# Earlier set-up, paired gates and early merge products in a transformer-layer kernel

## The chip, the cores and the metric

The kernel runs on one core of a Trainium2 chip. It is timed in microseconds of device time. The engines are TensorE (PE, matrix products), VectorE (DVE), ScalarE (ACT), GpSimd (POOL) and SyncE (SP, which here only issues DMAs).

## The reference

One layer of a trunk on an input of 512 x 1024 float32. The layer normalizes x to h, projects h by one matrix whose columns are shared by three branches and three gates, runs the branches, and merges them; an output projection and a gated feed-forward block follow. Cut to what matters here:

```python
h = rms_norm(x, g)
z = h @ w_in                       # columns: A (attention), B (S5), C (delta rule), gates
ya = dsa_attention(...) @ w_proj_a # index scores, top-k keys, attention
yb = s5_branch(...) @ w_proj_b     # complex diagonal scan: A_bar = exp(dt * a), B_bar from it
yc = gated_delta_rule(...) @ w_proj_c  # per chunk of 64: a triangular system is inverted
y = sum(sigmoid(gate_i) * y_i)     # the merge, a 512 x 1024 gate for each branch
x = x + y @ w_out
x = x + ffn(rms_norm(x, g2))
out = rms_norm(x, g_final)
```

Products are exact to about float32: each factor is split into a high and a low part of a reduced format (`wh`, `wl` and `hh`, `hl`), and three partial products are summed.

## The kernel before

**Products.** A product of 128 output columns is 8 slices of k by 3 partial products, that is 24 matmuls 128x512 (12 for a merge, whose k is 512). `wload` (L275 ff.) loads a weight tile by SyncE's queue into a staging tile `w` (two of them), casts it to `wh` on ScalarE (L258) and subtracts to `wl` on VectorE (L259). There are two pairs `wh`, `wl`; a third pair (`wx`) serves some of the 20 first products after the front. `proj` takes the next product from a queue of weights that are loaded up to three ahead. The PSUM tags are `acc` (2 buffers), `sm` (2), `pt` (3) and `po` (1).

**Order.** The program is written as generators (`topk`, `gates`, `s5_main`, `merge` and others) which strings and rates weave into one order. A scheduler with a model of the engines then orders each engine's queue; `issue_after` holds an instruction behind another in that order.

**Front.** Inputs come in by SyncE's queue. ScalarE and VectorE split the raw input into `xh`, `xl`; ScalarE squares x for the norm; the norm's factor goes through a power on GpSimd, a small product, and a copy on ScalarE to `rB`, one row broadcast to all partitions (L368). Four products of the raw input (`pu`), and a product of 76 columns for the index key (`index_in`, PSUM tag `acc`), need no norm; they are scaled by `rB` afterwards (L1448, L751). The normalized, transposed input is made in eight slices: `ht` by VectorE from `rB` (L1465), `hh` by ScalarE, `hl` by VectorE. Then come the gates: one product each, `m_th` = tanh of the accumulator by ScalarE (L1296), stored to `gd`. The set-up of S5 (`s5_setup`) is a generator of three steps: dt and the reduced angle; the magnitude, sine and cosine (L415 to L443) with a table load on ScalarE; and the discretized matrices. The first step stands before the products, the second is issued as the last weight of the front is there (`lastw`), the third follows in the weave.

**Exchange.** The delta rule inverts triangular blocks on VectorE, step by step (L928 to L938), writes the blocks to DRAM and gathers them block by block into `g_X` and its transpose `g_Y`, four gathers each, all on SyncE's queue (L959). The products from `g_X` (in tag `sm`) start the second level of the inverse. TensorE's filler around it are products of gates, and the first products of the merge of branch B (`merge`), which use the tag `acc`.

**Tail.** For each of four row blocks the sums of squares of the two halves are added, scaled, raised to −1/2 on GpSimd; ScalarE scales the first half, VectorE the second, and SyncE stores both.

Of the kernel before, what the change touches and what calls it, by code (L numbers as in the profile page):

```python
# [163 lines left out]
IL = 1  # L164
PI = 2
SE = 1
# [61 lines left out]
class _K:  # L228
# [46 lines left out]
    def wload(self, src, n=1024, hl=None, extra=False):  # L275
        nc = self.nc
        w = self.wp.tile([128, 1024], F32, tag="w", name="w", bufs=2)
        nc.sync.dma_start(w[:, :n], src)
        self.wi += 1
# [13 lines left out]
    def dense(self, ps, wh, wl, xh, xl, nk, c0=0, cs=128, m=128, t=slice(0, 512)):  # L293
        for k in range(nk):
# [4 lines left out]
            self.mm(ps[:, t], b, xh[:, k, t], False, k == nk - 1)  # L299
# [29 lines left out]
    def ahead(self, n):  # L329

        while len(self.fq) < n and self.fpos < len(PLAN):
# [3 lines left out]
            w = self.wload(self.I["w_in"][i], extra=self.fpos <= N_WX)  # L335
# [3 lines left out]
    def proj(self, i):  # L339
# [6 lines left out]
        return ps  # L346

# [38 lines left out]
    def s5_setup(self):  # L386
# [35 lines left out]
        tt(t1, t1, t1, OP.mult)  # L422
        nc.vector.tensor_scalar(cs, t1, -2.0, 1.0, OP.mult, OP.add)
# [57 lines left out]
    def s5_half(self, hf):  # L481
# [17 lines left out]
        E = self.s5e.tile([128, 8, 2, 64], F32, tag="b4", name="s5_b4", bufs=2)  # L499
        for ri, (x1, y1, x2, y2, op) in enumerate(((ar, bb[0], ai, bb[1], OP.subtract), (ar, bb[1], ai, bb[0], OP.add))):  # L500
# [3 lines left out]
            tt(e, e, u2, op)  # L504
        cre3 = v3("cre")
# [238 lines left out]
    def index_in(self, xh, xl):  # L744
# [3 lines left out]
        ps = self.acc()  # L748
# [46 lines left out]
    def gdn_main(self):  # L795
# [167 lines left out]
        for h0 in (0, 2):  # L963
            ps = self.acc("sm")
            P1 = [P1h(), P1h()]
            for h in range(2):
                nc.gpsimd.memset(half(P1[h], 1), 0.0)
                for t in range(4):
                    c = slice(t * 128, (t + 1) * 128)
                    o_ = h * 256 + t * 64  # L970
                    self.mm(ps[:, o_:o_ + 64], NT[:, h0 + h, c], half(XF[:, h0 + h, c], 0))
# [186 lines left out]
    def attn(self):  # L1158
# [17 lines left out]
        def keys(j):  # L1176
# [113 lines left out]
    def gates(self, n0, n1):  # L1290
        nc = self.nc
        for n in range(n0, n1):
            gd = self.dp.tile([128, 512], F32, tag="gd%d" % n, name="gd%d" % n, bufs=1)
            pg = self.proj(W_GA + n)
# [6 lines left out]
    def merge(self, wname, gate0, br, prev=None, dst=None):  # L1301
# [3 lines left out]
        for n2 in range(4):  # L1305
            ph, pl = self.wload(self.I[wname][n2])
            for j in range(2):
# [6 lines left out]
                ps = self.acc()  # L1314
                self.dense(ps, ph, pl, bh, bl, 4, c0=j * 512)
# [13 lines left out]
    def run(self):  # L1329
# [10 lines left out]
        self.gd, self.md = {}, {}  # L1340
        self.gpi, self.gpw = False, False
        self.wx, self.wi = None, 0
# [5 lines left out]
        with ExitStack() as mix:  # L1348
# [13 lines left out]
            with ExitStack() as s:  # L1362
                self.s5s = s.enter_context(self.pool("s5s", bufs=1))
# [18 lines left out]
                lsq, wst0 = [], []  # L1382

# [5 lines left out]
                def ld(c):  # L1389
# [25 lines left out]
                    else:  # L1415
                        with self.tc.issue_after(lsq[-1].ins) if lsq else ExitStack():
                            ws[n] = self.wload(I["w_in"][W_U + n])

                for i, c in enumerate(XO.split(',')):
                    ld(c)  # L1420
                    if i == PI:
                        sync(self.par[:, :64], I["par"][:, :64])
                        setup = self.s5_setup()
                        if SE == 0:
                            next(setup)
                sync(self.ident, I["const"][:, :128])
                if SE == 1:
                    next(setup)
# [15 lines left out]
                for n in range(4):  # L1444
                    if n % 2 == 0:
                        us = sqt()
# [3 lines left out]
                if SE == 2:  # L1450
                    next(setup)
# [5 lines left out]
                if not IL:  # L1457
                    self.index_in(xh, xl)
# [10 lines left out]
                if IL:  # L1469
                    self.index_in(xh, xl)  # L1470
# [3 lines left out]
                self.wx = s.enter_context(self.pool("wx", bufs=1))  # L1474
# [4 lines left out]
                drain(_weave(_chain(setup, self.s5_main()), fill, R_S5))  # L1479
# [184 lines left out]
```

## Time and profile before

| | us |
|---|---|
| median of 3 runs | 943.15 (941.37 to 944.28) |
| the profiled execution | 942.5 |
| its span | 940.7 |
| TensorE busy in it | 910.5 (97%) |
| VectorE busy | 642.9 (68%) |
| ScalarE busy | 415.3 (44%) |

The chain that ended last lies 77% of the span on TensorE, 12% on VectorE, 3% on ScalarE. The rows that the prediction uses stand in their own section below. In a row of a timeline the two first numbers are the start and the duration in microseconds; then come engine, line, operation, the tile written and the tiles read, the shape, a count, and in brackets how long the engine was idle before it and what released it. A matmul is pipelined, and starts before the one ahead has ended.

### The profile page before, as it was taken

Reading aid. Unit: us, or ns where it says so; the run is one execution under the profiler, and the core shown is the slowest. Engines: PE = TensorE matmul, PEld = TensorE weight load, DVE = VectorE, ACT = ScalarE, POOL = GpSimd, SP = SyncE. Lnnn points to the kernel's source line nnn. Section 1 sums busy time; section 2 is a strip of 40 time slices with the busy share of each in tenths; the row PEclk is TensorE's granted clock in tenths of the full one; section 3 lists DMA queues with packets and bytes.
Section 4 is the critical chain, followed back from the end, with each engine's and each line's share of the span. In section 5 each row is a group of like instructions: output and inputs, shape, how many; then the busy total and the mean of one; then the engine's idle time right before and its main releaser. Section 6 shows DMA issues by size and latency. Waiting matters only on the chain.

```text
span 940.7 us, 12731 instructions
## 1 busy us (share of the span) xinstructions
PE 910.5 (97%) x4804; PEld 744.1 (79%) x4804; DVE 642.9 (68%) x1132; ACT 415.3 (44%) x753; POOL 59.5 (6%) x99
## 2 busy tenths in 40 slices
PE   8899999998999999899999999999999999999996
PEld 6677877787888787788777889888888888888885
DVE  5879889789998779347678545866666666522423
ACT  6475453335575643258744224543444344321212
POOL 2221001110003100200100000000000000000000
PEclk9999999999999999899999999999999999999999
DMA  8485234532225545532137513422322322232312
GB/s 325 147 203 175 73 101 124 154 139 101 90 91 153 148 120 178 134 131 73 46 127 233 210 45 113 134 90 90 111 91 90 108 93 90 90 112 90 96 61 90
DMA packets 49677, 114.55 MB, mean 122 GB/s; under 512 B 15696, under 2 KB 16080, under 8 KB 49488
## 3 DMA queue, kind: packets, MB, share of 16 engines
q1 hardware_dynamic: 42256, 97.74, 32.1%
q0 software_dynamic: 3904, 9.70, 4.3%
q10 hardware_dynamic: 3456, 6.29, 1.8%
q8 instruction: 38, 0.62, 0.3%
q14 instruction: 23, 0.19, 0.1%
HBM read 94.84 MB, written 14.42 MB: 116 GB/s over the span
## 4 chain that ended last, share of the span: by engine, by line
PE 77%; DVE 12%; issue 3%; ACT 3%; DMA 3%; SPq 0%; POOL 0%; ACTq 0%; POOLq 0%; DVEq 0%
PE ps_acc L250 40%; PE ps_sm L250 20%; PE ps_pt L250 11%; PE ps_po L250 4%; DVE a_wk L1111 1%; DVE wl L259 1%; PE ps_pt L253 1%; DVE a_m L1110 1%; PE ps_sm L253 1%; DMA w<-in_w_in_dram 1%; ACT wh L258 1%; DMA xt<-in_xt_dram 1%; DVE ht L1465 1%; DVE s_rb L688 0%; DMA s_yT<-s_yd 0%
## 5 line engine op out<-in xcount | busy, mean ns | idle before, releaser
L259 DVE TENSOR_TENSOR wl<-w,wh 128x1024 fp32r<-128x1024 f32 (+1 forms) x140 | 168.8, 1207 | 142.9 <-ACT wh L258 142.8
L258 ACT CAST wh<-w 128x1024 fp32r<-128x1024 f32 (+1 forms) x140 | 145.4, 1039 | 220.8 <-PE ps_acc L250 120.1
L250 PE MATMUL ps_acc<-hh,wh 128*128 128x512 f32 x376 | 150.8, 401 | 5.4 <-ACT m_th L1296 2.8
L250 PE MATMUL ps_acc<-hh,wl 128*128 128x512 f32 x376 | 148.6, 396 | 0.9 <-DVE wl L259 0.9
L250 PE MATMUL ps_acc<-hl,wh 128*128 128x512 f32 x376 | 148.2, 395 | 1.0 <-DVE hl L259 1.0
L250 PEld LDWEIGHTS ps_acc<-hh,wh 128*128 128x128 f32 x376 | 71.1, 189 | 22.6 <-ACT m_th L1296 4.0
L250 PEld LDWEIGHTS ps_acc<-hh,wl 128*128 128x128 f32 x376 | 71.0, 189 | 17.1 <-DVE wl L259 1.3
L250 PEld LDWEIGHTS ps_acc<-hl,wh 128*128 128x128 f32 x376 | 71.1, 189 | 15.9 <-DVE hl L259 1.5
L250 PE MATMUL ps_acc<-f_hh,wh 128*128 128x512 f32 x160 | 62.3, 389 | 0.0
L250 PE MATMUL ps_acc<-f_hl,wh 128*128 128x512 f32 x160 | 62.3, 389 | 0.0
L250 PE MATMUL ps_acc<-f_hh,wl 128*128 128x512 f32 x160 | 62.2, 389 | 0.0
L250 PE MATMUL ps_sm<-f_hh,wh 128*128 128x512 f32 x160 | 62.2, 389 | 0.0
L250 PE MATMUL ps_sm<-f_hl,wh 128*128 128x512 f32 x160 | 62.2, 389 | 0.0
L250 PE MATMUL ps_sm<-f_hh,wl 128*128 128x512 f32 x160 | 62.2, 389 | 0.0
L258 ACT CAST ah<-f_th 128x512 fp32r<-128x512 f32 x22 | 13.6, 620 | 57.6 <-DVE f_th L1600 57.6
L250 PEld LDWEIGHTS ps_acc<-f_hh,wl 128*128 128x128 f32 x160 | 30.0, 188 | 6.3
L250 PEld LDWEIGHTS ps_sm<-f_hh,wh 128*128 128x128 f32 x160 | 30.0, 188 | 6.3
L250 PEld LDWEIGHTS ps_acc<-f_hh,wh 128*128 128x128 f32 x160 | 30.1, 188 | 6.2
L250 PEld LDWEIGHTS ps_sm<-f_hl,wh 128*128 128x128 f32 x160 | 30.1, 188 | 6.2
L250 PEld LDWEIGHTS ps_sm<-f_hh,wl 128*128 128x128 f32 x160 | 30.0, 188 | 6.2
L250 PEld LDWEIGHTS ps_acc<-f_hl,wh 128*128 128x128 f32 x160 | 30.0, 187 | 6.1
L1598 ACT ACTIVATE f_th<-f_a 128x512 f32<-128x512 f32 x22 | 13.9, 633 | 45.2 <-DVE f_a L1595 45.2
(538 smaller groups left out, 1944.7 us busy)
## 6 DMA issues: line engine op xcount, KB each, us to landing
w<-in_w_in_dram SPq DMA_DIRECT2D x50, 512.0 KB, 3.4
w<-in_w_up_dram SPq DMA_DIRECT2D x44, 512.0 KB, 3.4
w<-in_w_down_dram SPq DMA_DIRECT2D x22, 512.0 KB, 3.2
gd<-m_th ACTq DMA_DIRECT2D x24, 256.0 KB, 2.7
m_th<-gd SPq DMA_DIRECT2D x24, 256.0 KB, 3.2
w<-in_w_out_dram SPq DMA_DIRECT2D x8, 512.0 KB, 4.0
sq<-in_x_dram SPq DMA_DIRECT2D x4, 512.0 KB, 9.5
w<-in_w_proj_b_dram SPq DMA_DIRECT2D x4, 512.0 KB, 3.6
```

What stands on the lines that cost most here:

```text
L250: return self.nc.tensor.matmul(out, lhsT, rhs, start=start, stop=stop)
L253: return self.nc.tensor.transpose(out, in_, self.ident[base:base + n, base:base + n])
L258: self.lasta = nc.scalar.copy(hi, src)
L259: self.lastv = nc.vector.tensor_sub(lo, src, hi.bitcast(F32))
L1110: nc.vector.max(m8, wk[:, :N])
L1111: nc.vector.match_replace(wk[:, :N], m8, wk[:, :N], SENT)
L1465: nc.vector.scalar_tensor_tensor(h, xs[k // 2][:, k % 2], ag[:, k:k + 1], self.rB, OP.mult, OP.mult)
L1598: nc.scalar.activation(th, tl[0], AF.Tanh)
```

## The change

- `s5_setup`: the second step stands right behind the first inputs. Its magnitude no longer waits for the front's weights, its sines stand behind the third square of x, and half the angle's sine has a tile of its own. The third step is issued behind the last slice of h.
- A third pair of weight tiles (`wx`) exists from the start and serves the third front weight and the gates 0, 3, 6 and so on; every third staging tile comes from a pool of its own (`w3`).
- The two first gates are one function, `proj_pair`, which goes through k once for both.
- The index product accumulates in the tag `sm`, and stands behind the slices of h; the scaled `pu` products are stored two before and two behind it.
- Exchange: the gathers of `g_Y` go by GpSimd's queue; the zeros of the attention keys (`a_kl`) stand behind them; the first three products of the first merge accumulate in `pt`, and the first products from `g_X` are held behind them.
- Tail: the scale and the small constant are applied to the first half's sum when it is there, and the second half is added in one step; the first half of the output is shared by ScalarE (352 columns, its own DMA) and VectorE (160).

```diff
@@ wload
-        w = self.wp.tile([128, 1024], F32, tag="w", name="w", bufs=2)
+        self.wi += 1
+        if self.w3 and self.wi % 3 == 0:
+            w = self.w3.tile([128, 1024], F32, tag="w3", name="w", bufs=1)
+        else:
+            w = self.wp.tile([128, 1024], F32, tag="w", name="w", bufs=2)
         nc.sync.dma_start(w[:, :n], src)
-            if self.wx and extra and self.fpos % 3 == 0:
+            if self.wx and extra:
@@ ahead
-            w = self.wload(self.I["w_in"][i], extra=self.fpos <= N_WX)
+            w = self.wload(self.I["w_in"][i], extra=self.fpos <= N_WX and self.fpos % 3 == 1)
+    def proj_pair(self, i):
+        self.ahead(2)
+        two, pss = [self.fq.pop(0) for _ in range(2)], [self.acc(), self.acc()]
...
+        for k in range(8):
+            c = slice(k * 128, k * 128 + 128)
+            for ps, q in zip(pss, two):
+                wh, wl = q[1]
+                self.mm(ps, wh[:, c], self.hh[:, k], k == 0, False)
+                self.mm(ps, wl[:, c], self.hh[:, k], False, False)
+                self.mm(ps, wh[:, c], self.hl[:, k], False, k == 7)
+        self.ahead(3)
+        return pss
@@ s5_setup
-        with self.tc.issue_after(self.lastw.ins):
-            tt(t0, dt, P("are"), OP.mult)
-        with self.tc.issue_after(self.lastp.ins), self.tc.issue_after(self.lastw.ins):
-            exact_exp(mag, t0)
-        sn, cs = st("sn"), st("cs")
-        with self.tc.issue_after(self.lasta.ins):
+        tt(t0, dt, P("are"), OP.mult)
+        exact_exp(mag, t0)
+        sn, cs, hs = st("sn"), st("cs"), st("hs")
+        with self.tc.issue_after(self.lsq[2].ins):
             nc.scalar.activation(sn, r, AF.Sin)
-        nc.scalar.activation(t1, r, AF.Sin, scale=0.5)
+        nc.scalar.activation(hs, r, AF.Sin, scale=0.5)
@@ index_in
-        ps = self.acc()
+        ps = self.acc("sm")
@@ exchange
-                nc.sync.dma_start(g16(F)[s, :, s], xd[z][b].rearrange("g i k -> i g k"))
+                self.lastx = (nc.sync, nc.gpsimd)[z].dma_start(g16(F)[s, :, s], xd[z][b].rearrange("g i k -> i g k"))
...
+            with self.tc.issue_after(self.lastm[2].ins):
+                for h in range(2):
+                    for t in range(4):
+                        c = slice(t * 128, (t + 1) * 128)
+                        o_ = h * 256 + t * 64
+                        self.mm(ps[:, o_:o_ + 64], NT[:, h0 + h, c], half(XF[:, h0 + h, c], 0))
@@ attention keys
-                    nc.gpsimd.tensor_scalar(kl[z][o], self.C("ones")[o, 0:1].broadcast_to([64, 512]), 0.0, None, OP.mult)
+                    with self.tc.issue_after(self.lastx.ins):
+                        nc.gpsimd.tensor_scalar(kl[z][o], self.C("ones")[o, 0:1].broadcast_to([64, 512]), 0.0, None, OP.mult)
@@ gates
-            pg = self.proj(W_GA + n)
+            if n == 0:
+                two = self.proj_pair(W_GA)
+            pg = two.pop(0) if two else self.proj(W_GA + n)
@@ merge
-                ps = self.acc()
-                self.dense(ps, ph, pl, bh, bl, 4, c0=j * 512)
+                ps = self.acc("pt" if not prev and not dst and n < 3 else "acc")
+                self.lastm.append(self.dense(ps, ph, pl, bh, bl, 4, c0=j * 512))
@@ run, front
+                self.w3 = s.enter_context(self.pool("w3", bufs=1))
+                self.wx = s.enter_context(self.pool("wx", bufs=1))
...
-                            ws[n] = self.wload(I["w_in"][W_U + n])
+                            ws[n] = self.wload(I["w_in"][W_U + n], extra=n == 2)
...
-                if SE == 1:
-                    next(setup)
+                next(setup)
+                next(setup)
...
-                if IL:
-                    self.index_in(xh, xl)
+                self.index_in(xh, xl)
+                us = sqt()
+                for n in range(2, 4):
+                    scale_u(n, us)
+                with self.tc.issue_after(self.lasth[1].ins):
+                    next(setup)
...
-                drain(_weave(_chain(setup, self.s5_main()), fill, R_S5))
+                drain(_weave(_chain((1, 1), self.s5_main()), fill, R_S5))
@@ tail
-                nc.vector.tensor_tensor(fss[:, t:t + 1], fss[:, t:t + 1], fss[:, 4 + t:5 + t], OP.add)
-                self.rstd(frs[:, t:t + 1], fss[:, t:t + 1], 1024.0, 1)
+                ms = fss[:, t:t + 1]
+                nc.vector.scalar_tensor_tensor(ms, fss[:, 4 + t:5 + t], 1.0 / 1024.0, fss[:, 8 + t:9 + t], OP.mult, OP.add)
                 rs = frs[:, t:t + 1]
+                nc.gpsimd.tensor_tensor(rs, ms, self.mhalf[:, 0:1], OP.pow)
-                nc.scalar.activation(ys[t], ys[t], AF.Identity, scale=rs)
-                nc.sync.dma_start(dst[:, :512], ys[t])
+                c = 352
+                nc.scalar.activation(ys[t][:, :c], ys[t][:, :c], AF.Identity, scale=rs)
+                nc.scalar.dma_start(dst[:, :c], ys[t][:, :c])
...
+                nc.vector.tensor_scalar(ys[t][:, c:], ys[t][:, c:], rs, None, OP.mult)
+                nc.sync.dma_start(dst[:, c:512], ys[t][:, c:])
```

What the scheduler makes of it is seen in each engine's order. ScalarE's queue at the front, from the squares of x (`sq`) on, before; `s_sn` is the sine, `wh` with 608 columns the index weight:

```order
L1402 ACTIVATE sq,ssq<-sq 128x1024 x3
L258 CAST wh<-w 128x1024
L1402 ACTIVATE sq,ssq<-sq 128x1024
L1491 CAST rsel<-cst 128x16
L258 CAST wh<-w 128x1024
L258 CAST wh<-w 128x608
L420 ACT_TABLE_LOAD
L420 ACTIVATE s_sn<-s_r 128x16
L368 COPY rB<-ps_sm 128x512
```

and after, where `s_hs` is the sine of half the angle:

```order
L1433 ACTIVATE sq,ssq<-sq 128x1024 x2
L437 ACT_TABLE_LOAD
L437 ACTIVATE s_hs<-s_r 128x16
L1433 ACTIVATE sq,ssq<-sq 128x1024
L436 ACTIVATE s_sn<-s_r 128x16
L256 CAST wh<-w 128x1024
L1433 ACTIVATE sq,ssq<-sq 128x1024
L256 CAST wh<-w 128x1024
L1520 CAST rsel<-cst 128x16
L256 CAST wh<-w 128x608
L386 COPY rB<-ps_sm 128x512
```

The table load and the sines have moved from behind the index weight to a place between the squares, so that `rB` follows the index weight directly.

TensorE's queue at the first two gates, before (`ps_acc_500` is gate 0, and the number tells the accumulators and weights apart):

```order
L250 MATMUL ps_acc_500<-hl_84,wh_496 128x512
L250 MATMUL ps_acc_500<-hh_83,wl_497 128x512
L250 MATMUL ps_acc_500<-hh_83,wh_496 128x512
L250 MATMUL ps_acc_500<-hl_84,wh_496 128x512
L250 MATMUL ps_acc_500<-hh_83,wl_497 128x512
L250 MATMUL ps_acc_500<-hh_83,wh_496 128x512
L253 MATMUL ps_sm_410<-ident_66,ik_404 128x12 x4
L250 MATMUL ps_acc_558<-hh_83,wh_527 128x512
```

and after, where `ps_acc_521` is gate 0 and `ps_acc_522` gate 1:

```order
L248 MATMUL ps_acc_521<-hh_83,wh_511 128x512
L248 MATMUL ps_acc_521<-hh_83,wl_512 128x512
L248 MATMUL ps_acc_522<-hh_83,wh_517 128x512
L248 MATMUL ps_acc_521<-hl_84,wh_511 128x512
L248 MATMUL ps_acc_521<-hh_83,wh_511 128x512
L248 MATMUL ps_acc_521<-hh_83,wl_512 128x512
L248 MATMUL ps_acc_521<-hl_84,wh_511 128x512
L248 MATMUL ps_acc_521<-hh_83,wh_511 128x512
L248 MATMUL ps_acc_521<-hh_83,wl_512 128x512
L248 MATMUL ps_acc_521<-hl_84,wh_511 128x512
L248 MATMUL ps_acc_522<-hh_83,wl_518 128x512
L248 MATMUL ps_acc_522<-hl_84,wh_517 128x512
```

Gate 0 stood alone for 19 matmuls, six slices and one more; now the two gates take turns, and both end at the pair's end.

TensorE's queue at the first use of the gathered blocks, before (`f_h`, `f_l` are the factors of a merge, `g_X` the blocks):

```order
L250 MATMUL ps_acc<-f_l,wh 128x512
L250 MATMUL ps_acc<-f_h,wl 128x512
L250 MATMUL ps_acc<-f_h,wh 128x512
L250 MATMUL ps_acc<-f_l,wh 128x512
L250 MATMUL ps_acc<-f_h,wl 128x512
L250 MATMUL ps_sm<-g_X,g_NT 128x64 x8
L250 MATMUL ps_acc<-f_h,wh 128x512
L250 MATMUL ps_acc<-f_l,wh 128x512
```

and after, where `a_ch` and `a_wkh` belong to the attention keys and values:

```order
L248 MATMUL ps_pt<-f_h,wl 128x512
L248 MATMUL ps_pt<-f_h,wh 128x512
L248 MATMUL ps_pt<-f_l,wh 128x512
L248 MATMUL ps_pt<-f_h,wl 128x512
L248 MATMUL ps_acc<-a_ch,a_wkl 128x512
L248 MATMUL ps_acc<-wh,a_ch 128x512
L248 MATMUL ps_acc<-wl,a_ch 128x512
L248 MATMUL ps_acc<-wh,a_cl 128x512
L248 MATMUL ps_sm<-g_X,g_NT 128x64 x8
L248 MATMUL ps_acc<-f_h,wh 128x512
L248 MATMUL ps_acc<-f_l,wh 128x512
```

The first three merge products, 36 matmuls in `ps_pt`, stand ahead of the blocks now, where 12 of one product in `ps_acc` stood, and key and value products are mixed in with them.

## Rows read from the trace of the kernel before

**Rows 1.** Page, part 1: engine, busy us (share of the span), instructions.

```profile
PE 910.5 (97%) x4804; PEld 744.1 (79%) x4804; DVE 642.9 (68%) x1132; ACT 415.3 (44%) x753; POOL 59.5 (6%) x99
```

**Rows 2.** Windows: us, busy per engine, then PEclk, DMA share, GB/s.

```profile
47.00:51.00 4.00, 3.99 (x13) 3.24 (x14) 4.00 (x11) 3.07 (x8) 3.49 (x10) 0.57 0.56 133
58.00:62.00 4.00, 4.00 (x19) 3.28 (x19) 1.89 (x6) 3.04 (x7) 0.00 (x0) 1.00 0.99 202
379.00:385.00 6.00, 6.00 (x23) 5.42 (x24) 0.76 (x2) 0.00 (x0) 3.36 (x4) 0.50 0.68 165
```

**Rows 3.** Timeline of TensorE, first gates: start, us, what, [idle before <- releaser].

```profile
39.55 0.39 PE L250 MATMUL ps_acc<-hh,wh 128*128 128x512 f32 x1
...
55.42 0.40 PE L250 MATMUL ps_acc<-hh,wl 128*128 128x512 f32 x1
...
57.76 0.50 PE L250 MATMUL ps_acc<-hh,wh 128*128 128x512 f32 x1 [1.95 <-ACT m_th L1296]
...
75.36 0.50 PE L250 MATMUL ps_acc<-hh,wh 128*128 128x512 f32 x1 [0.88 <-ACT m_th L1296]
```

**Rows 4.** Timeline of TensorE, from the solve to the use of X.

```profile
330.64 0.50 PE L250 MATMUL ps_acc<-hh,wh 128*128 128x512 f32 x1
...
371.05 0.40 PE L250 MATMUL ps_acc<-hh,wl 128*128 128x512 f32 x1
...
372.99 0.50 PE L250 MATMUL ps_acc<-f_h,wh 128*128 128x512 f32 x1 [1.54 <-DVE g_k L788]
...
378.77 3.65 PE L250 MATMUL ps_sm<-g_X,g_NT 128*128 128x64 f32 x16 [2.75 <-DMA g_X<-g_xd]
```

**Rows 5.** Timeline of ScalarE, 20 to 58 us.

```profile
20.20 1.05 ACT L258 CAST wh<-w 128x1024 fp32r<-128x1024 f32 x1 [1.98 <-PE ps_acc L250]
...
29.83 0.57 ACT L368 COPY rB<-ps_sm 128x512 f32<-128x512 f32 x1
...
54.75 1.05 ACT L258 CAST wh<-w 128x1024 fp32r<-128x1024 f32 x1 [4.68 <-issue]
55.82 1.28 ACT L1296 ACT_TABLE_LOAD   x1
57.11 0.60 ACT L1296 ACTIVATE m_th<-ps_acc 128x512 f32<-128x512 f32 x1
```

**Rows 6.** Timeline of VectorE, 21 to 48 us.

```profile
21.28 1.23 DVE L259 TENSOR_TENSOR wl<-w,wh 128x1024 fp32r<-128x1024 f32 x1 [3.76 <-ACT wh L258]
...
30.43 2.02 DVE L1448 TENSOR_TENSOR sq<-ps_acc,rB 128x512 f32<-128x512 f32 x2 [1.21 <-ACT rB L368]
...
39.60 0.18 DVE L429 TENSOR_TENSOR s_ai<-s_mag,s_sn 128x16 f32<-128x16 f32 x1
...
47.65 0.68 DVE L259 TENSOR_TENSOR hl<-ht,hh 128x512 fp32r<-128x512 f32 x1
```

**Rows 7.** Timeline of GpSimd, the power of the first norm.

```profile
22.66 1.09 POOL L352 TENSOR_TENSOR nir<-rs,mhalf 128x4 f32<-128x4 f32 x1 [12.27 <-DVE rs L351]
```

**Rows 8.** Timeline of VectorE, start and end of the triangular solve.

```profile
339.25 0.16 DVE L928 TENSOR_TENSOR g_xt<-g_W,g_ND 128x1 f32<-128x1 f32 x1 [3.22 <-DMA g_ND<-g_nd]
...
372.24 0.69 DVE L788 SCALAR_TENSOR_TENSOR g_k<-g_k,ps_acc 128x512 f32<-128x512 f32 x1
```

**Rows 9.** Timeline of the DMA queue of SyncE (SPq), the gathers of X.

```profile
375.21 1.92 SPq L959 DMA_DIRECT2D g_X<-g_xd  x4
```

**Rows 10.** DMA issues: tiles, queue, count, KB each, us to landing.

```profile
s_U<-s_ud POOLq DMA_DIRECT2D x4, 256.0 KB, 5.0
```

**Rows 11.** Windows of two later stretches.

```profile
194.00:297.00 103.00, 100.45 (x468) 82.12 (x468) 100.42 (x218) 56.31 (x143) 7.62 (x14) 1.00 0.30 99
380.00:474.00 94.00, 91.04 (x670) 76.10 (x670) 56.27 (x164) 56.63 (x156) 5.38 (x4) 0.97 0.29 91
```

**Rows 12.** Timeline of the end of the program.

```profile
934.64 0.16 DVE L1609 TENSOR_TENSOR fss<-fss 128x1 f32<-128x1 f32 x1
...
935.64 0.72 ACT L1613 ACTIVATE f_y<-f_y,frs 128x512 f32<-128x512 f32 x1 [1.03 <-POOL frs L352]
```

More of the change, by code (lines that the diff above doesn't have):

```diff
@@ L163 @@
 TA = 1
-IL = 1
 PI = 2
-SE = 1
 PO = 'a'
@@ L298, in dense @@
             self.mm(ps[:, t], a, xl[:, k, t], False, False)
-            self.mm(ps[:, t], b, xh[:, k, t], False, k == nk - 1)
+            r = self.mm(ps[:, t], b, xh[:, k, t], False, k == nk - 1)
+        return r
     def dense_halves(self, ws, tags):
@@ L346, in proj @@
         return ps
+    def proj_pair(self, i):
+        self.ahead(2)
+        two, pss = [self.fq.pop(0) for _ in range(2)], [self.acc(), self.acc()]
+        assert [q[0] for q in two] == [i, i + 1]
+        self.lasta, self.lastv = two[1][2:]
+        for k in range(8):
[7 more added lines that the diff above has]
+        return pss
     def rstd(self, dst, ssq, n, width, extra=1.0):
@@ L499, in s5_half @@
         E = self.s5e.tile([128, 8, 2, 64], F32, tag="b4", name="s5_b4", bufs=2)
+        held = ExitStack()
+        if hf == 0:
+            held.enter_context(self.tc.issue_after(self.lasth[1].ins))
         for ri, (x1, y1, x2, y2, op) in enumerate(((ar, bb[0], ai, bb[1], OP.subtract), (ar, bb[1], ai, bb[0], OP.add))):
@@ L504, in s5_half @@
             tt(e, e, u2, op)
+        held.close()
         cre3 = v3("cre")
@@ L967, in gdn_main @@
                 nc.gpsimd.memset(half(P1[h], 1), 0.0)
[L968 to L971, printed above, removed]
+            with self.tc.issue_after(self.lastm[2].ins):
[4 more added lines that the diff above has]
+                        self.mm(ps[:, o_:o_ + 64], NT[:, h0 + h, c], half(XF[:, h0 + h, c], 0))
             for h in range(2):
@@ L1291, in gates @@
         nc = self.nc
+        two = []
         for n in range(n0, n1):
             gd = self.dp.tile([128, 512], F32, tag="gd%d" % n, name="gd%d" % n, bufs=1)
-            pg = self.proj(W_GA + n)
+            if n == 0:
+                two = self.proj_pair(W_GA)
+            pg = two.pop(0) if two else self.proj(W_GA + n)
             th = self.mp.tile([128, 512], F32, tag="mt", name="m_th", bufs=3)
@@ L1339, in run @@
         nc.gpsimd.memset(self.mhalf, -0.5)
-        self.gd, self.md = {}, {}
+        self.gd, self.md, self.lastm = {}, {}, []
         self.gpi, self.gpw = False, False
-        self.wx, self.wi = None, 0
+        self.wx, self.w3, self.wi = None, None, 0
         self.fq, self.fpos = [], 0
@@ L1382, in run @@
                 lsq, wst0 = [], []
+                self.lsq = lsq
                 nc.gpsimd.memset(self.rB, 0.0)
@@ L1443, in run, with scale_u @@
                 jc = lambda e: e.rearrange("p (c j) -> p j c", j=4)
-                for n in range(4):
-                    if n % 2 == 0:
-                        us = sqt()
+                def scale_u(n, us):
                     uv = us[:, (n % 2) * 512:(n % 2) * 512 + 512]
@@ L1449, in run @@
                     nc.gpsimd.dma_start(self.ud[n * 128:(n + 1) * 128], uv)
-                if SE == 2:
-                    next(setup)
+                us = sqt()
+                for n in range(2):
+                    scale_u(n, us)
                 sync(self.par[:, 64:], I["par"][:, 64:])
@@ L1456, in run @@
                 sync(self.cst, I["const"][:, 128:N_KEEP])
-                if not IL:
-                    self.index_in(xh, xl)
                 for k in range(8):
@@ L1468, in run @@
                         self.lasth = (self.lasta, self.lastv)
-                if IL:
-                    self.index_in(xh, xl)
+                self.index_in(xh, xl)
+                us = sqt()
+                for n in range(2, 4):
+                    scale_u(n, us)
+                with self.tc.issue_after(self.lasth[1].ins):
+                    next(setup)
                 self.dump("hT", self.hh.bitcast(F32), self.hl.bitcast(F32))
@@ L1473, in run @@
                 self.s5 = s.enter_context(self.pool("s5", bufs=1))
-                self.wx = s.enter_context(self.pool("wx", bufs=1))
                 drain(self.s5_uu())
@@ L1478, in run @@
                 fill = _order(ORD, {"t": tk, "g": gt})
-                drain(_weave(_chain(setup, self.s5_main()), fill, R_S5))
+                drain(_weave(_chain((1, 1), self.s5_main()), fill, R_S5))
                 drain(fill)
-                self.wx = None
+                self.wx = self.w3 = None
                 self.gpw = GE > 0
@@ L1636, in fin_ @@
                         ys[t] = y
+                        nc.vector.tensor_scalar(fss[:, 8 + t:9 + t], fss[:, t:t + 1], 1.0 / 1024.0, EPS, OP.mult, OP.add)
                     else:
```

9 lines of the change are left out of this document (3 added, 6 removed).

## The prediction

> **What bounds the kernel now.** I read the table of busy time first: TensorE is busy 97% of the span of 940.7 us [rows 1], so a change that leaves the products alone can only win back its waits and its half-clock stretches. The waits of TensorE by releaser come next; the two largest entries are the tanh that empties a gate's accumulator and the gathered inverse blocks, and their rows stand below at their places in the timeline. Then the windows: the granted clock is 0.57 at 47 to 51 us and 0.50 at 379 to 385 us, but 1.00 at 58 to 62 us [rows 2], that is 1.2 GHz in (part of) the two bad places and 2.4 GHz otherwise. Ahead of both, TensorE had stood still. Last I read the timelines of the engines at these places.
>
> At the front the first gate begins at 39.55 us, right behind the last set-up product; the second gate's last product starts at 55.42 us, and the third gate only at 57.76 us, behind a wait of 1.95 us for a tanh [rows 3]. In the middle, the products behind the last piece of the solve's set-up start at 330.64 us; TensorE waits 1.54 us at 372.99 and 2.75 us at 378.77 us for the inverse blocks X [rows 4]. Between 330.64 and 371.05 us lie 177 dense matmuls, so one takes (371.05 − 330.64) / 176 = 0.23 us from start to start [rows 4].
>
> **Front: table load, set-up, index product.** ScalarE has 1.98 us idle ahead of the cast at 20.20 us [rows 5], VectorE 3.76 us ahead of the subtraction at 21.28 us [rows 6]. The change puts the Sin table load (1.28 us, as the load at 55.82 [rows 5]), two small Sin activations and some ten small VectorE steps of at most 0.18 us [rows 6] into these two idle times, and a power into a time in which GpSimd idles 12.27 us [rows 7]. I cost them at nothing; without that cover they would push the third weight cast by up to 1.7 us. What leaves ScalarE's queue is a load of 1.28 us ahead of the copy rB at 29.83 us [rows 5]; VectorE's first use of rB, at 30.43 us, waits for that copy [rows 6]. So rB comes about 1.3 us earlier, and VectorE's chain of scaled tiles with it. The chain ran from 30.43 to 48.33 us [rows 6], 17.9 us. The index product's scaling and three weight subtractions are still in it after the change; the small set-up steps, about 1.1 us together, are not. Its last tile lands between 46.0 and 47.4 us.
>
> **Front: the pair of gates.** Before, gate 0 asks for a new scaled tile every three matmuls and overtakes VectorE. From 39.55 to the end of gate 1 at 55.65 us (55.42 and a last step) 16.1 us go by [rows 3], where 48 matmuls and four small transposes (0.45 us) need 48 × 0.23 + 0.45 = 11.5 us. The other 4.6 us are waits and the half clock. With the two gates interleaved by k, a new tile is asked for every six matmuls, 1.38 us: the last one at about 39.2 + 41 × 0.23 = 48.6 us, later than 47.4, so I expect no wait for a tile. (39.2: the set-up products start some 0.35 us earlier, since the third weight tile no longer waits for a free pair.) The pair ends at 39.2 + 11.5 = 50.7 us.
>
> What is late next is the tanh. The cast of gate 3's weights stands ahead of it on ScalarE and waits for gate 0's pair. Before, that cast started at 54.75 us, about a step behind the start of gate 0's last matmul, and the third gate started 3.01 us later: cast 1.05, load 1.28, tanh 0.60, and gaps [rows 5, 3]. After, gate 0's last matmul is the last but one of the pair, 39.2 + 46 × 0.23 + 0.45 = 50.2 us; the cast starts at 50.4 and the third gate at 53.4 us, **−4.35 us** against 57.76. TensorE then waits 2.7 us there instead of 1.95. Bounds: −7.1 (no wait there at all) and −1.3 (the longer wait brings a half-clock stretch, priced at 3.05 us below).
>
> The Trainium skill ("ScalarE: Activation LUTs", section "What ACT_TABLE_LOAD costs") counts a drain of about 1.38 us on top of a load of about 1.28 us at each switch of table. The trace agrees on the load, 1.28 us at 55.82, but shows no drain behind it: the tanh starts at 57.11 us, 1.29 us after the load's start [rows 5]. An estimate by the page would put the third gate of the changed kernel 1.4 us later, and the sum 1.4 us higher; I go by the rows.
>
> Behind the front, TensorE waits 0.88 us at 75.36 us for a tanh [rows 3], where the third pair of tiles and the earlier Sin steps have reordered ScalarE. I take **−0.9**; for the reshuffled S5 stretch as a whole the bounds are −3 and +3, about three such waits either way.
>
> **Exchange.** X comes from VectorE's triangular solve. Its first step starts at 339.25 us behind a transfer [rows 8], 8.6 us behind the landmark 330.64; X's gathers are issued at 375.21 us [rows 9], and X is used at 378.77, 48.1 us behind the landmark. By the order of TensorE 198 dense matmuls stand between landmark and X where 189 stood, so TensorE reaches X 198 × 0.23 = 45.5 us behind the landmark. On VectorE two convolution steps of 0.69 us [rows 8] and one key subtraction move into the solve, +1.8 us with gaps: X lands at 48.1 + 1.8 = 49.9 us. The wait is 4.4 us in one piece, where it was 1.54 + 2.75 = 4.3 us in two. The merge products mostly take the place of other filler: 156 gate matmuls stand there instead of 177. I take **0**, bounds +1.8 and −7.5 (rival A). The half clock stays with the wait: 379 to 385 us ran 6 us at 0.50 [rows 2], and so it costs 6.1 / 2 = 3.05 us.
>
> Y's gathers now stand on GpSimd's queue, behind memsets that are done long before. GpSimd's gathers of the S5 inputs land 5.0 us after issue [rows 10]; with four issues Y lands some 4 us behind X, and is used some 9 us behind it. I cost that at nothing, bounds 0 and +2. The key zeros queued behind them wait for Y's issue; their readers, the attention scores, come later still.
>
> **Behind the exchange.** The three merge products used early are missing as filler. From 380 to 474 us TensorE is busy 91.04 of 94 us and VectorE 56.27 [rows 11]: 3 us are idle already, and attention and scan wait for each other there. I take **+1.2**, bounds 0 and +10 (rival C).
>
> **Tail.** The addition of the two sums at 934.64 us and the scaling behind it become one step (about −0.2), and the last activation, 0.72 us [rows 12], shrinks to 352 of 512 columns (about −0.15): **−0.35**, bounds 0 and −0.6.
>
> **Sum.** −4.35 − 0.9 + 0 + 1.2 − 0.35 = −4.4 us. The profiled execution took 942.5 us (the span and 1.8 us around it); 942.5 − 4.4 = 938.1. The median of the runs lies 0.65 us over the profiled one, which gives **938.7 us**.
>
> **Rivals.** A difference under 0.3% (2.8 us) can't be told from none here, so faster means below 940.3 and slower above 946.0 us.
>
> *A, the wait for X goes too.* If the solve starts earlier relative to TensorE, by 4.4 us or more, X is there when TensorE is: 4.4 us of wait and 3.05 of half clock go, 938.7 − 7.5 = 931.2 us. For it: the order puts more of TensorE's work ahead of the landmark, and if VectorE gets ahead meanwhile, the two added steps and the casts between the solve's steps fall away. Against it: the solve starts behind a transfer that follows TensorE's own landmark, so an earlier front moves both.
>
> *B, the front's gain is eaten by VectorE.* From 194 to 297 us VectorE is busy 100.42 of 103 us [rows 11], and its last scaled tile lands hardly earlier than before (47.4 against 48.33 us). If its queue reaches 194 us at the old time, the 4.35 and 0.9 us turn into waits there and only the tail is left: 942.5 + 0.65 − 0.35 = 942.8 us. Against it: VectorE idles at 21 and 30 us [rows 6] and after, and can catch up.
>
> *C, slower.* Behind the exchange the filler runs out: 36 merge matmuls, 36 × 0.23 = 8.3 us, are used before X, and attention and scan go at the pace of VectorE and ScalarE. Waits of 1.5 to 2.8 us were followed by the half clock at 379 us; two more such spells are 6.1 us, and half of the lost cover is 4.1 us: 10.2 us, against 5.6 us gained elsewhere. That gives 943.15 − 5.6 + 10.2 = 947.8 us, and it is slower than before from the point where the stretch loses more than 5.6 us. Against it: all those products are done in any case, and the wait of 1.95 us at 57.76 was followed by a clock of 1.00 [rows 2, 3].
>
> **How the numbers follow.** Forecast 0.53 (own range 935.5 to 941.5), A 0.17, B 0.17, C 0.13. Faster: 0.44 of the forecast, A, and 0.03 of B, 0.64; same: 0.09, 0.13 of B and 0.02 of C, 0.24; slower: 0.11 of C and 0.01 of B, 0.12. The range goes from 931 to 944.5 us: it takes in the forecast, B and the nearer half of A, and leaves out C.
>
> **What would show it.** Right: no half clock between 39 and 51 us; the copy rB at about 28.5 us; the third gate's first matmul at about 53.4 us, behind one wait for a tanh of some 2.7 us; a wait for X of 4 to 5 us with half clock behind it. Wrong: a wait for a scaled tile inside the pair, half clock behind the third gate's wait, no wait for X (A), TensorE waiting for VectorE between 194 and 297 us (B), or new waits and a clock well under 1.00 between 390 and 474 us (C).

## The result, and the profile after

The changed kernel takes 937.75 us (median of 4 runs, 937.33 to 938.35) where the kernel before took 943.03 beside it; the ratio is 0.9949 with a 95% interval of 0.9930 to 0.9967. Predicted were 938.7 us in a range of 931 to 944.5: faster, by the forecast's size. The profiled execution took 937.33 us, its span is 935.5. Medians and ratios here are of fast runs; two slow ones, of no_pair (1817.3 us, the profiled one) and of the kernel before (1509.83 us), are left out.

First the windows of the changed kernel over the stretches of [rows 2, 11]; columns as there.

```profile
53.00:57.00 4.00, 3.63 (x10) 2.91 (x11) 4.00 (x6) 1.75 (x3) 0.51 (x1) 0.64 1.21 201
60.00:194.00 134.00, 132.45 (x945) 103.10 (x944) 105.19 (x174) 66.17 (x100) 10.39 (x21) 1.00 0.41 124
194.00:297.00 103.00, 102.45 (x473) 83.11 (x472) 101.06 (x215) 58.41 (x147) 10.99 (x19) 1.00 0.34 108
380.00:474.00 94.00, 90.18 (x686) 75.91 (x687) 60.33 (x176) 59.03 (x165) 11.62 (x10) 0.96 0.30 87
```

The granted clock falls in a new place (a mean of 0.64 over 53 to 57 us), and in the stretch from 380 us TensorE is nearly as busy as before (90.18 against 91.04 us). The timelines of ScalarE and TensorE at the front, answering [rows 5, 3]:

```profile
28.32 0.59 ACT L386 COPY rB<-ps_sm 128x512 f32<-128x512 f32 x1 [3.06 <-PE ps_sm L248]
...
50.36 1.04 ACT L256 CAST wh<-w 128x1024 fp32r<-128x1024 f32 x1 [1.66 <-PE ps_acc L248]
51.42 1.28 ACT L1324 ACT_TABLE_LOAD   x1
52.72 0.60 ACT L1324 ACTIVATE m_th<-ps_acc 128x512 f32<-128x512 f32 x1
```

```profile
53.37 0.50 PE L248 MATMUL ps_acc<-hh,wh 128*128 128x512 f32 x1 [2.85 <-ACT m_th L1324]
53.71 0.39 PE L248 MATMUL ps_acc<-hl,wh 128*128 128x512 f32 x1
53.94 0.43 PE L248 MATMUL ps_acc<-hh,wl 128*128 128x512 f32 x1
54.17 0.63 PE L248 MATMUL ps_acc<-hh,wh 128*128 128x512 f32 x1
54.59 0.63 PE L248 MATMUL ps_acc<-hl,wh 128*128 128x512 f32 x1
```

The third gate starts at 53.37 us, and no wait for a scaled tile stands inside the pair. But from 54.17 to 57.6 us the matmuls behind the wait start 0.43 us apart instead of 0.23, the half clock (1.2 GHz): eight steps, 1.6 us. At the exchange [rows 4], TensorE of the changed kernel:

```profile
378.76 0.50 PE L248 MATMUL ps_acc<-wl,a_ch 128*128 128x512 f32 x1 [0.36 <-DVE wl L257]
379.10 0.39 PE L248 MATMUL ps_acc<-wh,a_cl 128*128 128x512 f32 x1
381.88 3.65 PE L248 MATMUL ps_sm<-g_X,g_NT 128*128 128x64 f32 x16 [2.39 <-DMA g_X<-g_xd]
385.28 0.77 PE L248 MATMUL ps_acc<-f_h,wh 128*128 128x512 f32 x1
385.85 0.63 PE L248 MATMUL ps_acc<-f_l,wh 128*128 128x512 f32 x1
386.28 0.63 PE L248 MATMUL ps_acc<-f_h,wl 128*128 128x512 f32 x1
```

The wait for X and the half clock behind it (steps of 0.43 us) are still there. The table below sums up where the time went. It is worked out from all matmul records: TensorE's loss in a stretch is the stretch less its matmuls, each counted with the median step of its shape in the kernel before; "step" is the mean step between neighbouring 128x512 matmuls from 60 to 365 us (990 to 1026 in each kernel). Each row is one profiled execution, so differences of a few tenths say nothing. The first 20 us are left out: they differ by up to 2.7 us between the profiles, five of which have half clock at some 11 to 15 us and the others not.

```
loss, us          20-60   60-80  80-360 360-400 400-480 480-600   step, us
before             8.75    1.29   22.98    8.33    6.15    2.62     0.2293
changed            6.43    0.17   24.51    7.31    4.17    2.66     0.2331
tanh_table_early   3.45   -0.16   21.53    7.30    4.00    1.59     0.2283
after_shift32      3.94   -0.16   21.84    8.72    4.12    1.49     0.2283
no_pair_again      5.11    0.17   24.57    1.21    4.56    3.54     0.2331
hold_x_4th         5.55    0.16   24.88    4.18    4.57    2.65     0.2331
front_only         6.31    0.02   22.08    7.14    5.27    2.43     0.2300
exchange_only      7.50    1.66   23.00    0.88    4.94    2.51     0.2293
tail_only          8.79    2.04   25.33    6.67    5.76    2.69     0.2332
before_shift64     7.24    3.98   22.46    8.87    6.00    1.69     0.2287
all_together       2.93    1.79   21.98    5.25    4.79    1.63     0.2284
```

Two rows explain the result. The changed kernel gains 2.3, 1.1, 1.0 and 2.0 us, and loses 1.5 us from 80 to 360 us, although it waits less there (TensorE is busy 102.45 us from 194 to 297, where it was busy 100.45 [rows 11]). Its dense matmuls run at 0.2331 us a step instead of 0.2293, 3.8 ns on 1011 of them, which is 3.8 us. Nothing in the prediction speaks of that. The columns 60-80 and 80-360 belong together: 64 products of 16 columns stand ahead of 80 us in the changed kernel and behind it before, and by the step that they are counted at, up to 0.9 us moves from one column to the other. Together the two say 0.4 us lost.

### The profile page after: what moved, and what is told of

It reads as the page before. It is cut to its first block, busy times and chain, and to the rows that moved or that the text cites. A ratio compares the mean times of both kernels' runs of the same rounds, so it can differ in the third digit from the quotient of the medians.

```text
span 935.5 us, 12723 instructions
## 1 busy us (share of the span) xinstructions
PE 914.2 (98%) x4804; PEld 744.2 (80%) x4804; DVE 646.1 (69%) x1136; ACT 414.4 (44%) x753; POOL 62.7 (7%) x103
## 4 chain that ended last, share of the span: by engine, by line
PE 84%; DVE 9%; issue 3%; DMA 2%; ACT 1%; SPq 1%; POOL 0%; POOLq 0%; DVEq 0%; ACTq 0%
PE ps_acc L248 43%; PE ps_sm L248 22%; PE ps_pt L248 13%; PE ps_po L248 4%; DVE wl L257 1%; PE ps_pt L251 1%; DMA sq<-in_x_dram 1%; PE ps_sm L251 1%; DMA w<-in_w_glu_dram 1%; DVE g_xt L958 1%; DVE g_W L959 1%; DVE a_p L1256 0%; DVE s_rd L710 0%; DVE ht L1491 0%; DVE hl L257 0%
## 5 line engine op out<-in xcount | busy, mean ns | idle before, releaser
L256 ACT CAST ah<-f_th 128x512 fp32r<-128x512 f32 x22 | 13.6, 620 | 57.6 <-DVE f_th L1629 57.6
```

The lines of the kernel that those rows point to most:

```text
L256: self.lasta = nc.scalar.copy(hi, src)
```

## The experiments

**Index product and pair.** Three kernels ask what makes the first two gates quick. The edit of idx_in_sm_only, on the kernel before, and its opposite (idx_in_acc, on the changed one):

```diff
-        ps = self.acc()
+        ps = self.acc("sm")
         self.dense(ps[:76], wh, wl, xh, xl, 8, cs=76, m=76)
```

> The kernel before with one edit: the index product accumulates in tag sm instead of acc. Theory P (what the first two gates gain comes from taking turns in the program and from the earlier scaled tiles): the scheduler may interleave the gates here too, but the last scaled tile still lands at about 48.3 us and rB at about 30.4, so the third gate starts no earlier than 56.5 us and the time is 942.4 (941.7 to 943.1) us. Theory R (the index product held one of the two accumulators acc until its scaling was done, so gate 1 could not start; once it is in sm the scheduler itself lets the gates take turns): waits for tiles and the half clock at 47 to 51 us go, third gate at about 54 us, 940.0 (939 to 941) us.

Measured: 942.9 us, ratio 1.0009 (0.9995 to 1.0024). The gates behave as theory R said (third gate at 54.40 us, clock 1.00 from 40 to 52 us), and the time is the one of theory P:

```profile
54.40 0.79 PE L250 MATMUL ps_acc<-hh,wh 128*128 128x512 f32 x1 [2.40 <-ACT m_th L1296]
52.00:60.00 8.00, 5.60 (x18) 4.51 (x19) 4.23 (x8) 5.02 (x9) 1.02 (x2) 0.79 1.10 232
```

(A timeline row, and a window as above.) TensorE's loss from the start to 200 us is 34.2 us, where it was 34.35 before. Two things eat the gain: the half clock, behind the third gate and again behind waits for VectorE's scan steps (0.66 over 173 to 178 us), and those waits, which are longer than before (`s_sr` 1.4 us instead of 0.9, `s_si` 1.1 instead of 0.8, `s_rc` 1.0 instead of 0.5). The longer waits are the mechanism of the prediction's rival B, seen in a kernel that moves the gates and not the set-up; they are only part of the loss.

> The changed kernel with the index product back in acc. Theory P: the paired gates keep their gain, 938.0 (937.3 to 938.7) us. Theory R: gate 1 can't start until the index product's scaling has freed the accumulator; gate 0 runs ahead alone and waits for scaled tiles again, with half clock behind it: third gate 2 to 3 us later than 53.4, 940.3 (939.5 to 941.5) us.

Measured: 939.05 us, ratio 0.9964 (0.9952 to 0.9975), between the two ranges. The waits for tiles came back, as R said, but without the half clock that R put behind them (1.00 over 40 to 60 us), and the third gate came 2.5 us later; TensorE of idx_in_acc:

```profile
43.21 0.50 PE L248 MATMUL ps_acc<-hl,wh 128*128 128x512 f32 x1 [1.41 <-DVE hl L257]
...
45.73 0.50 PE L248 MATMUL ps_acc<-hh,wh 128*128 128x512 f32 x1 [0.62 <-ACT hh L256]
...
55.91 0.50 PE L248 MATMUL ps_acc<-hh,wh 128*128 128x512 f32 x1 [2.39 <-ACT m_th L1324]
```

The index product's accumulator is thus what let gate 0 run ahead alone. Of the 2.5 us the medians show 1.3 (the intervals of the two kernels overlap); one reason in the profile is that here the third gate has no half clock behind it.

no_pair takes the two gates back to separate calls:

```diff
-            if n == 0:
-                two = self.proj_pair(W_GA)
```

> The changed kernel with the two first gates as two calls of proj instead of proj_pair, all else as it is. Theory P: gate 0 asks for a tile every three matmuls, waits come back inside the gates, about +2.5 us: 940.3 (939.5 to 941.5) us. Theory R: the scheduler lets them take turns anyway, 937.8 (937.0 to 938.6) us, third gate at 53 to 54 us with one wait.

Measured: 930.75 us (three runs), ratio 0.9874 (0.9853 to 0.9896): 7 us faster than the changed kernel, which neither theory said. no_pair_again is the same kernel, profiled.

> The kernel of no_pair a second time, for a profile at the usual clock. Its order has 215 matmuls ahead of X instead of 198. Theory A: 17 x 0.23 = 3.9 us more filler, no wait for X and no half clock behind it, about 6 us, and at the front the third gate's wait is short of 2 us without half clock: 930.8 (930 to 932) us. Rival (it gains only at the front): wait for X of 2 us or more in the profile, and the gain all before 200 us.

Measured: 932.92 us, ratio 0.9892 (0.9871 to 0.9912), 0.9 us above theory A's range. At the front the gates take turns as theory R said (one wait, none for a tile), but the third gate's wait is 2.39 us and not short of 2, and the half clock follows it (a mean of 0.79 over 52 to 60 us), which theory A did not expect. The gain is at the exchange, 1.21 us of loss instead of 7.31; TensorE at the third gate and there:

```profile
54.10 0.50 PE L248 MATMUL ps_acc<-hh,wh 128*128 128x512 f32 x1 [2.39 <-ACT m_th L1322]
...
378.58 0.40 PE L248 MATMUL ps_acc<-a_ch,a_wkl 128*128 128x512 f32 x1
378.81 0.78 PE L248 MATMUL ps_sm<-g_X,g_NT 128*128 128x64 f32 x6
379.40 0.48 PE L248 MATMUL ps_acc<-wh,a_ch 128*128 128x512 f32 x1
```

No wait for X and no half clock (1.00 over 378 to 384 us): this is what the prediction's rival A describes, whose time was 931.2 us. It comes here from more filler, and not from an earlier solve.

**The exchange by itself.** front_only and exchange_only apply one part of the change to the kernel before (its edits as in the diff above, the other parts left out).

> The kernel before with the exchange part of the change alone (Y's gathers on GpSimd, key zeros behind them, three merge products in pt ahead of X); front and tail as before. Its order has 216 matmuls ahead of X where 189 stood. Theory A (filler decides): 27 x 0.23 = 6.2 us more of it cover the waits of 1.54 and 2.75 us, no half clock: 943.0 - 4.3 - 3.05 = 935.7 (934.5 to 937) us. Rival (prediction's step: filler added only replaces other filler, wait and half clock stay): 943.0 (942 to 944) us.

Measured: 936.62 us, ratio 0.9935 (0.9919 to 0.9951): theory A. Loss from 360 to 400 us falls from 8.33 to 0.88, and the clock stays up there; window of exchange_only, against 0.50 in [rows 2]:

```profile
379.00:385.00 6.00, 6.00 (x38) 5.20 (x37) 2.77 (x6) 2.32 (x4) 5.68 (x7) 1.00 0.84 226
```

> The kernel before with the front part of the change alone (set-up earlier, third pair of weight tiles, paired gates, index product in sm); exchange and tail as before. Its order has 36 merge matmuls (in acc) ahead of X all the same, 195 matmuls in all. Theory E (the exchange edits give nothing; front's gain of 4 us up to 80 us, and the filler order that follows from the front's numbers): 937.8 (936.8 to 939) us, wait for X of 2 to 4 us with half clock. Rival (the 2 us won between 400 and 480 us come from the merge products in pt and from the key zeros behind Y's gathers): 939.8 (939 to 941) us.

Measured: 935.79 us, ratio 0.9940 (0.9917 to 0.9963), faster than both theories said; its twelve runs spread from 932.9 to 943.1 us, more than those of any other kernel here. The loss from 400 to 480 us falls by 0.9 us with the front alone and by 1.2 with the exchange alone, so the 2 us belong to neither part by itself. Its wait moved: 3.42 us for VectorE's `g_k` step at 373.02, with half clock behind it (0.50 over 372 to 376 us), instead of the wait for X.

```profile
373.02 0.79 PE L248 MATMUL ps_acc<-f_h,wh 128*128 128x512 f32 x1 [3.42 <-DVE g_k L809]
```

So each part alone gives what both together give. Of the kernels with the exchange edits, those with separate gates have 215 or 216 matmuls ahead of X, the changed one 198, and only the former cover the wait for X. hold_x_4th puts 12 more there by hand:

```diff
-            with self.tc.issue_after(self.lastm[2].ins):
+            with self.tc.issue_after(self.lastm[3].ins):
```

> The changed kernel with the first products from X held behind the fourth merge product instead of the third: 12 more matmuls ahead of X, 210 instead of 198, and nothing else in TensorE's order up to there. Theory A (rival A of the prediction: the wait for X and the half clock behind it are one price, paid because filler runs out about 2.8 us before X lands): TensorE reaches X 2.8 us later and finds it there; wait 0 to 0.3 us, no half clock, 5 to 5.8 us less than 937.75: 932.4 (931.5 to 933.5) us. Rival (filler moved ahead of X is missing behind it): the wait goes but comes back between 385 and 480 us, 936 to 938 us.

Measured: 935.5 us, ratio 0.9921 (0.9905 to 0.9937, which just meets the changed kernel's interval), between theory A's range and the rival's. The wait for X and the half clock went (1.00 over 381 to 387 us), as theory A said, but about half of the gain came back, as the rival said, in small waits ahead of X and behind it: loss from 360 to 400 us is 4.18, not 1.2. The scheduler also put ScalarE's and VectorE's steps there into another order, so filler is not the only thing that this kernel changes.

```profile
381.75 0.50 PE L248 MATMUL ps_acc<-f_h,wh 128*128 128x512 f32 x1 [0.68 <-ACT a_V L1224]
...
389.15 0.50 PE L248 MATMUL ps_acc<-wh,a_ch 128*128 128x512 f32 x1 [1.19 <-DVE m_th L1344]
```

**The third gate's wait.** tanh_table_early loads the table while ScalarE idles:

```diff
-        nc.scalar.copy(self.ab.rearrange("p a b -> p (a b)"), pt[:, :48])
+        ab = nc.scalar.copy(self.ab.rearrange("p a b -> p (a b)"), pt[:, :48])
+        pre = self.sm.tile([128, 1], F32, tag="pre", name="m_pre", bufs=1)
+        with self.tc.issue_after(ab.ins):
+            nc.scalar.activation(pre, self.mhalf[:, 0:1], AF.Tanh)
```

> The changed kernel with a tanh of one column put on ScalarE behind the copy ab, so that the table load stands in ScalarE's idle time ahead of gate 3's cast instead of between it and the tanh. The rest of each engine's order is the same. Theory S (the half clock at 54 to 57.6 us follows from the length of the wait ahead of it): third gate at 52.1 us behind 1.7 us of waiting, no half clock, 1.28 + 1.6 = 2.9 us less: 934.9 (934.2 to 936.0) us. Rival (what the front gains is given back by VectorE between 80 and 200 us): the gates come earlier but the time stays at 937.2 to 938.2 us. Second rival (the half clock comes however long the wait is): 936.5 us.

Measured: 931.09 us, ratio 0.9882 (0.9865 to 0.9900). The third gate came at 52.05 us behind 1.44 us of waiting, without half clock (1.00 over 52 to 57 us), and the loss from 20 to 60 us fell by 2.98 us, as theory S said. That the shorter wait kept the clock up is not shown: after_shift32 below has no half clock there either, behind a wait as long as the changed kernel's. The time is 3.8 us under theory S's 934.9: the other 3.7 us lie from 60 us on, nearly all behind 80, where every engine's order is the same as in the changed kernel. TensorE of the changed kernel, and then of tanh_table_early at the third gate and from about 300 us:

```profile
299.81 0.40 PE L248 MATMUL ps_acc<-hh,wl 128*128 128x512 f32 x1
...
301.21 0.39 PE L248 MATMUL ps_acc<-hh,wl 128*128 128x512 f32 x1
```

```profile
52.05 0.50 PE L248 MATMUL ps_acc<-hh,wh 128*128 128x512 f32 x1 [1.44 <-ACT m_th L1327]
...
299.81 0.39 PE L248 MATMUL ps_acc<-hh,wl 128*128 128x512 f32 x1
...
301.40 0.39 PE L248 MATMUL ps_acc<-hh,wh 128*128 128x512 f32 x1
```

Six steps take 1.40 us in the one (0.233 each), seven take 1.59 in the other (0.227). What differs is where tiles lie: the new tile of one column moves all that is allocated behind it by 32 bytes.

**The tiles' place.** By the programs that the kernels build, the two weight pairs start, within a partition, at 32 modulo 128 bytes in the kernel before, at 64 in the changed one (its `fss` grew by 16 bytes, and tiles are placed in units of 32), at 96 in tanh_table_early; `hh` and `hl` lie at 96 in every kernel. Two kernels get an unused tile, with the order of all else unchanged. Such a tile moves every tile of the pools behind it, the weights among them:

```diff
         nc.gpsimd.memset(self.mhalf, -0.5)
+        pad = self.sm.tile([128, 8], F32, tag="pad", name="pad", bufs=1)
+        nc.gpsimd.memset(pad, 0.0)
```

(8 columns in after_shift32, 16 in before_shift64.)

> The changed kernel with one unused tile of 32 bytes per partition in the pool sm, so that all tiles of the pools that follow (the weight pairs among them) lie 32 bytes further, at 96 modulo 128 bytes instead of 64; every other instruction and its order are the same. Theory M (the step between dense matmuls hangs on where the weight tiles lie: 0.2331 us on average at 64 in the changed kernel, 0.2282 at 96 in tanh_table_early, between 60 and 365 us): steps of 0.227 to 0.229 us, half clock at 54 us as in the changed kernel, 3.3 us less between 60 and 360 and 1.2 behind: 933.3 (932.3 to 934.5) us. Rival (tanh_table_early's gain beyond 2.9 us came with the earlier gates): 937.8 (937.0 to 938.6) us, steps of 0.233 us.

Measured: 933.11 us, ratio 0.9892 (0.9879 to 0.9906), as theory M said. The step fell to 0.2283 us. One thing was unexpected: the wait ahead of the third gate is the same as in the changed kernel, and the clock behind it stayed up, in the one execution that was profiled, so 1.6 us of its 4.6 may be that.

```profile
54.20 0.51 PE L248 MATMUL ps_acc<-hh,wh 128*128 128x512 f32 x1 [2.85 <-ACT m_th L1324]
54.54 0.40 PE L248 MATMUL ps_acc<-hl,wh 128*128 128x512 f32 x1
54.77 0.40 PE L248 MATMUL ps_acc<-hh,wl 128*128 128x512 f32 x1
```

> The kernel before with an unused tile of 64 bytes per partition in sm: its weight tiles move from 32 to 96 modulo 128 bytes. Theory M: steps between dense matmuls go from 0.229 to 0.227 between 60 and 365 us and from 0.233 to 0.227 between 500 and 590: 2.4 + 1.2 us less, 939.4 (938.3 to 940.6) us. Rival: no difference, 943.0 (942.3 to 943.7) us.

Measured: 941.01 us, ratio 0.9985 (0.9975 to 0.9995): a gain, but half of what M said; the mean step fell by 0.6 ns only, not by 2. The traces show why: the products with the two moved pairs went from 0.2292 to 0.2278 us a step, but the third pair `wx` moved too, from 96 to 32, and its products went from 0.2285 to 0.2335. Its profile also has half clock where the kernel before has none (3.98 us lost from 60 to 80 us, 1.29 before).

> The kernel before with the tail part alone. Its tile fss grows from 32 to 48 bytes per partition, which moves all weight tiles from 32 to 64 modulo 128 bytes, as in the changed kernel. Theory M: steps of 0.233 instead of 0.229 us between 60 and 365 us, some 2.6 us more, and nothing won at the end: 945.4 (944.4 to 946.6) us. The prediction's term for the tail: 942.7 (942.3 to 943.1) us. From the last sum (the last fss) to the end of the span: 6.06 us before and 6.2 in the changed kernel; the prediction's term says 5.7.

Measured: 943.0 us, ratio 1.0002 (0.9993 to 1.0012): no change, inside the range of the prediction's tail term and under M's. The step rose to 0.2332 us, as M said; the time did not follow. Part of it is that a slower step eats waits where TensorE waits anyway: the loss from 360 to 400 us fell by 1.7. So a quicker step took 3 to 4.6 us off the changed kernel (after_shift32), and a slower one added nothing to the kernel before.

**All together** joins no_pair and tanh_table_early, and with the latter's tile the tiles' place.

> The changed kernel with three of the edits tried so far: the gates as two calls of proj (215 matmuls ahead of X), the early tanh table load, and by its one-column tile the weight tiles at 96 modulo 128 bytes. If the three gains add: from 931.8 (no_pair's two medians) 2.9 for the third gate and 4.5 for the tiles' place are to come off: 924.4 (923 to 927) us; no wait for X, third gate at about 52 us without half clock, steps of 0.227 to 0.229. If they share a cause, 929 to 931 us.

Measured: 930.09 us, ratio 0.9846 (0.9828 to 0.9864), the best ratio of all, but 5.7 us above the sum of the gains (924.4) and 3 us above the top of its range. The gains do not add: with the third gate at 51.4 us, TensorE waits for VectorE's S5 steps from 60 us on (2.4 us for `s_sr`, 1.3 for `s_ks`), and 360 to 400 us cost 5.25 us, because X comes without a wait but TensorE then waits 1.45 us at 377.75 us for an attention step of VectorE (`a_mx`), with half clock behind that (0.54 over 379 to 385 us). It beats the kernel before and the changed one clearly; its interval meets that of no_pair.

## Why the prediction was right, and where not

- **The front's order.** Right to 0.2 us: rB at 28.32 us (said: 28.5), the last scaled tile at 47.07 (46.0 to 47.4), the third gate at 53.37 (53.4), the wait 2.85 (2.7). By this the table load costs its 1.28 us and no drain, as the trace of before showed. The term was mis-sized by the half clock behind the wait, which the prediction had as a bound and as a sign of being wrong: 1.6 us of the 4.35 went.
- **What did it.** The prediction gave the paired gates the credit, and here its mechanism was wrong. no_pair shows that the scheduler lets the gates take turns by itself once the index product is out of `acc`; idx_in_acc shows the waits coming back without that.
- **The wait at 75.36 us.** The wait of 0.88 us is gone, as said (0.9).
- **From 80 to 360 us.** Said: no change; measured: 1.5 us lost (0.8 if the small products are counted the other way). The step that failed is the assumption that a dense matmul takes the 0.23 us of [rows 4] in both kernels: 3.8 ns more on 1011 matmuls, less some waits that went. after_shift32 shows that it hangs on the tiles' place and gives back 2.7 us in this stretch. Rival B's absorption was not seen in the changed kernel, but in part in idx_in_sm_only.
- **Exchange.** The wait stayed and the half clock with it, as said; X was used 49.3 us behind the landmark (332.59 us; said: 49.9), the wait was 2.39 and 0.36 us instead of 4.4 because TensorE got there later than 45.5 us (at 46.9; 198 steps of 3.5 ns more are 0.7 us of that). "The merge products take the place of other filler" holds for the whole change only. exchange_only and no_pair show that they do add filler, and take 6 to 7 us off the loss there, when the gates are not paired.
- **Behind the exchange.** Said: +1.2; measured: −2.0. The step that failed is the sign: the order there gained instead of running out of filler. Each part alone gives about half of it (0.9 us in front_only, 1.2 in exchange_only); which instruction does it stays open.
- **Tail.** Said: −0.35; measured: nothing. From the last `fss` step to the end of the span 6.06 us became 6.2 (5.9 in tail_only). The steps did get shorter, and the last output DMA is issued 0.19 us earlier behind that step, but it lands no earlier, 4.2 us behind it in both: three output DMAs stand where two were. That they are the cause was not tried.

The errors cancelled: +1.6 (half clock), +1.5 (step) and +0.5 (tail) against −1.0 (exchange) and −3.2 (behind it). So the times at the front were foreseen, but that the whole time came out within 1 us of the forecast is luck.

## What to carry to other kernels

When two edits each gain alone, run both alone before the sum is believed: here the pair of gates takes away the filler that the exchange needed, and the change without the pair is 5 to 7 us faster. Count the filler between a transfer's source and its use in the built order; the wait and the clock behind it are one price. After any change of a tile's size, compare the step between dense matmuls: some bytes in a small tile can move every tile behind it.

## What was not expected of the hardware

- The step between dense 128x512 matmuls at full clock is not one number, and it hangs on where tiles lie. With the instructions in the same order, the changed kernel's products of `hh` and `hl` with the two weight pairs take 0.2332 us a step with the pairs at 64 modulo 128 bytes, and 0.2278 with the pairs at 96 (after_shift32). Over all kernels of this document they take 0.228 us at 96, 0.229 at 32 and 0.233 at 64.
- The weight tile alone does not decide it. In the output projection (from about 500 to 570 us) the weight tile `mh` lies at 96 in every kernel, and the step is 0.233 us where the moved tile lies at 32 or 64 and 0.227 where it lies at 96. From 600 us on, in the feed-forward, both tiles lie at the same place, whichever it is, and the step is 0.2267 us in every kernel. In these three groups the shortest step comes with both tiles at the same place modulo 128 bytes. It is not a full rule: `hh` with the third pair, both at 96, took 0.2285 us in the kernel before and 0.2324 in front_only. No kernel was built to test it.
- The clock behind a wait does not follow from the wait's length alone: ahead of the third gate 2.85 us were followed by half clock in the changed kernel and by full clock in after_shift32; 2.39 us by full clock in idx_in_acc and by a mean of 0.79 over 52 to 60 us in no_pair_again; 1.95 us by full clock in the kernel before [rows 2, 3] and by a mean of 0.57 over 59 to 63 us in exchange_only.
